# The second pair's gate products moved ahead of the first pair's down products in a mixer and mixture-of-experts layer

## The chip, the cores and the metric

One core of one Trainium2 chip runs the whole program. The metric is the device time of one launch in microseconds (us). Below, PE is TensorE (matrix products), DVE is VectorE, ACT is ScalarE, POOL is GpSimd, and SP is SyncE, which here only issues DMA transfers. Each engine works through its own instructions strictly in the order in which they are written to it.

## The reference

One layer over 1024 tokens of width 1024: a mixer (two kinds of gated linear attention), a layer norm, a mixture of experts, and a second layer norm. The change lies in the mixture of experts, cut here to what matters:

```python
p_top_group, g_idx = lax.top_k(softmax(x @ w_group_router), 1)       # 8 groups
p_top, e_local = lax.top_k(softmax(e_logits_of_that_group), 2)       # 2 of its 8 experts
gates = p_top_group * p_top / sum(p_top)
# for each of 64 experts e, over the rows of x that are sent to it:
h = silu(x_e @ w_gate[e]) * (x_e @ w_up[e])      # 1024 -> 512, twice
y += gates * (h @ w_down[e])                     # 512 -> 1024
out = layer_norm(ALPHA * x + y, ln2_g, ln2_b)
```

## The kernel before

The mixer, the first norm and the router fill the first 545 us. Then `pairs()` walks over the 64 experts in 32 pairs; a pair is two experts, each with up to 64 rows, side by side in the 128 rows of one tile. The six weight matrices of a pair are called units, 2 MB each: two gates (units 6p and 6p+1 of pair p), two ups (6p+2, 6p+3) and two downs (6p+4, 6p+5). All 192 units, 403 MB, come from HBM.

Ten units fit on the chip: four `w1u` and four `w2u` buffers that are used in turn for ever, and two `w3u` buffers (pools `preL` and `preR`) that hold only the first pair's downs, units 4 and 5. `load_after(i)` queues on SP the load that goes into the buffer of unit i, and SP waits there until PE's last product with unit i is done. So units 10 and 11 (second pair's downs) wait for the first pair's gate products, 12 and 13 (third pair's gates) for its ups, 14 and 15 for the second pair's gates, 16 and 17 for the second pair's ups, 18 and 19 for the second pair's downs. Behind units 4 and 5 nothing is loaded; the space of their two buffers is taken over, once the first pair's down products are done, by the pools `home` (tiles `parts` and `rest`) and `ring` (tiles `y`, `rows` and others).

PE's order is written out by hand (`tc.manual_schedule`); the other engines' order comes from the framework's scheduler, except where `order(a, b, ...)` puts a behind b on one engine. For one pair PE does:

- `gp`, the gate products: 16 instructions (8 chunks of the 1024 inputs for 2 experts), then ACT makes `sg` = silu of it;
- `up`, 16 more, then DVE multiplies `sg` by it;
- `hidden`: 4 transposes of `sg` into PSUM (name `tp`), which DVE copies to `hT`;
- `down`, two halves n = 0, 1 of 8 instructions, which ACT and DVE scale into `y` (`scaled`);
- `add_rows` of the pair before, 8 products that add its `y` to the sums of its group of 8 experts (name `cp`).

The rows `xt` of the first two pairs are fetched with an indirect DMA each (`gather`, into `xgs[2]` and `xgs[0]`) and turned on PE (`transposed`), and ACT writes the result. From the third pair on they are picked on PE from the group's rows (`picked`, 24 products a half), which are held as three bf16 tiles in `parts`. `split_rows(g, c, E)` makes these for class c of group g: ACT casts the first (`b0`), engine E subtracts it (`rest`), ACT casts the second (`b1`), E subtracts that into the third (`b2`). Small tables say which row is whose: `trow` and `grow` are spread over the partitions by one product each (`spread_out`), `first_rows` finds a group's first-class rows with three small products, and `adders` makes `adds` from `grow`. `spread` turns vectors of ln2 into the tiles `lns`; numbers 6 and 7 are made inside the first pair. Before the change the first pair was the first pass of the loop, with many `if p == 0`:

```python
            if p == 0:
                spread(6, ps_c, "cp")
                spread(7, ps_c, "cp")
            if p == 0:
                transposed(xgs[0], (0,))
            ...
            hT = hidden(sg)
            ...
                for c in range(4):
                    down(p, yps, hT, n, c)
```

Of the kernel before, what the change touches and what calls it, by code (L numbers as in the profile page):

```python
# [20 lines left out]
D = 1024  # L21
# [38 lines left out]
def mixer_moe_kernel(ctx: ExitStack, tc: tile.TileContext, x_in, xT_in, wf_in, wv_in, wvg_in, wa2_in,  # L60
# [1093 lines left out]
    def turned(products, halves):  # L1154

        xt = xts.rearrange("p (c s) -> p c s", c=KT)
# [9 lines left out]
    def transposed(src, halves=(0, 1)):  # L1166

        sv = src.rearrange("p (k c) -> p c k", c=KT)
        return turned(lambda o, c: PE.transpose(o, sv[:, c], ident), halves)
# [16 lines left out]
    def hidden(sg):  # L1186
# [6 lines left out]
        V.tensor_copy(hT, hp)  # L1193
# [55 lines left out]
    def spread_out(col, n, name, pool):  # L1249

        w = mw.tile([128, n, 128], F32, name="sg", bufs=1)
# [9 lines left out]
    def slot_tokens(g):  # L1261
        return spread_out(tokf[:, GP * g:GP * g + GP], GP, "trow", mw)

    def row_tokens(g):
        return spread_out(rtok[:, 2 * g:2 * g + 2], 2, "grow", ring)
# [8 lines left out]
    def first_rows(g):  # L1274

        tp = ps_x.tile([128, 1], F32, name="tp")
        for q in range(GP - 1):
            col = slice(GP * g + q, GP * g + q + 1)
            m = mw.tile([128, 128], F32, name="own")
# [15 lines left out]
    def split_rows(g, c, E):  # L1295
# [3 lines left out]
        rest = home.tile([128, KT, 128], F32, name="rest", bufs=1)  # L1299
        S.copy(b0, x)  # L1300
        o = E.tensor_tensor(rest, x, b0, OP.subtract)
        if g == 0:
            order(o, evacuated, "the sums of the pair before go first")
        S.copy(b1, rest)
        ends[g] = E.tensor_tensor(b2, rest, b1, OP.subtract)

# [65 lines left out]
    def pairs():  # L1372
# [6 lines left out]
        for p in range(npair):  # L1379
            g, q = divmod(p, GP)  # L1380
            if p == 0:
                gather(xgs[0], sidx[:, 1:2])
                fetch_rows(0, (1,))
            if p == 1:
                for c in (1, 0):
                    split_rows(0, c, V)
            if q == 1:
                for c in range(2):
                    order(gained(G, rows_of[g % 2, c]), ends[g], "the next group's rows go first")
                if g + 1 < NG:  # L1390
                    fetch_rows(g + 1)
            if q > 1 and g + 1 < NG:
                split_rows(g + 1, q - 2, G)
            if 0 < p < last:
# [10 lines left out]
            for u, dst in ((0, gp), (2, up)):  # L1405
                for c in range(KT):
                    if p == last and u == 2 and c == 0:
                        for n in range(2):
                            PE.matmul(sums[g][1][n], own[1], rows_of[g % 2, 1][:, n * 512:(n + 1) * 512], start=False,
                                      stop=False)  # L1410
                    for b in range(2):
                        PE.matmul(dst[64 * b:64 * b + 64], xt[:, c, 64 * b:64 * b + 64], utile[6 * p + u + b][:, c],  # L1412
                                  start=(c == 0), stop=(c == KT - 1))
                for b in range(2):
                    load_after(6 * p + u + b)
                if u == p == 0:
                    count_places()
                    first_rows(0)
                if u == 0:
                    sg = mw.tile([128, FF], F32, name="sg", bufs=1)  # L1420
                    silu = S.activation(sg, gp, AF.Silu)  # L1421
                    if p == last:
                        order(S.activation(mw.tile([128, 1], F32, name="zve"), one1, AF.Sqrt), silu, "one table, then the other")
                    elif p:
                        add_rows(p - 1, adds)
                    if p == last - 1:
                        order(G.drain(), outs[-1], "the rows that are complete go first")
            V.tensor_tensor(sg, sg, up, OP.mult)  # L1428
            if p == 0:
                spread(6, ps_c, "cp")  # L1430
                spread(7, ps_c, "cp")
            if p == 0:
                transposed(xgs[0], (0,))
            elif p < last:
                picked(picks, (0,))
            hT = hidden(sg)
            yps = [ps_g.tile([128, 512], F32, name="gu") if p else ps_c.tile([128, 512], F32, name="cp") for _ in range(2)]
            if 0 < p < last:
                ys[p] = ring.tile([128, 2, D], F32R, name="y")
            for n in range(2) if p < last - 1 else ():  # L1440
                for c in range(4):
                    down(p, yps, hT, n, c)
                if n == 0:
                    if p == 0:
                        xt = transposed(xgs[0], (1,))
                        fetch_rows(0, (0,))
                        trow[:] = [slot_tokens(0)]
                    else:
                        xt = picked(picks, (1,))
                    if q == 2 and g + 1 < NG:  # L1450
                        trow[:] = [slot_tokens(g + 1)]
                if p:
                    scaled(yps, n, gcol[:, p:p + 1], ys[p][:, 0], ys[p][:, 1])
            if p == 0:
                preL.release()
                preR.release()
# [227 lines left out]
```

## Time and profile before

| what | us |
|---|---|
| median of three runs | 1506.78 |
| lowest and highest of them | 1503.84, 1508.77 |
| the profiled execution | 1504.2 |
| its span, first to last instruction | 1502.4 |
| PE busy in it | 1436.2 |

The granted PE clock was 0.998 of full speed. The profile of one execution gives, beside busy times, a row of the 16 DMA engines' busy share in 40 equal slices of 37.6 us, and their throughput in GB/s; a timeline of each engine (start, duration, engine, line, operation, names, and in brackets the idle time before it with what ended it); and sums over stretches that one chooses. A row of the timeline merges like instructions that follow each other, and its duration runs from the first one's start to the last one's end; neighbouring rows overlap by up to 0.1 us, since an engine starts one instruction while the one before drains. An fp32 product of 512 columns counts as two records in the trace (x32 for 16 instructions).

### The profile page before, as it was taken

How to read it: one execution, taken by the hardware profiler on the slowest of the kernel's cores; microseconds unless marked ns; L12 is line 12 of the kernel's file. 1: busy time of each engine (PE TensorE's matmuls, PEld its weight loads, DVE VectorE, ACT ScalarE, POOL GpSimd, SP SyncE). 2: the span in 40 equal slices, each digit the busy share in tenths (PEclk: the TensorE clock that was granted, in tenths of full speed). 3: DMA queues.
4: the chain of work that ended last, by engine and by line, in shares of the span. 5: the costliest groups of instructions: out<-in, count | busy, mean ns of one | idle time of the engine just before them, and what ended most of it. 6: DMA issues, size and time to landing. Idle time of an engine off the chain costs nothing. (4 is left out here: it accounts for less than half of the span.)

```text
span 1502.4 us, 24758 instructions
## 1 busy us (share of the span) xinstructions
PE 1436.2 (96%) x10397; PEld 834.5 (56%) x10397; DVE 627.2 (42%) x1476; ACT 488.6 (33%) x961; POOL 223.2 (15%) x164
## 2 busy tenths in 40 slices
PE   9999999999999999999999999999999999999996
PEld 7888788887888854334344444444343443444432
DVE  6776674838545865141151132133033133114213
ACT  6656553557322423311311311221222221231120
POOL 0000000010012213220320220140140130032000
PEclk9999999999999999999999999999999999999999
DMA  5111111101285278999999999999999999999995
GB/s 184 50 37 43 30 36 37 30 29 45 80 319 198 113 270 356 416 427 427 426 426 427 426 428 424 428 426 425 428 427 428 425 427 427 426 428 425 425 420 213
DMA packets 58293, 445.50 MB, mean 297 GB/s; under 512 B 8916, under 2 KB 17364, under 8 KB 32576
## 3 DMA queue, kind: packets, MB, share of 16 engines
q1 hardware_dynamic: 51184, 430.01, 69.1%
q0 software_dynamic: 4896, 8.84, 1.6%
q10 hardware_dynamic: 2096, 5.01, 0.9%
q8 instruction: 83, 1.36, 0.4%
q14 instruction: 34, 0.28, 0.0%
HBM read 440.24 MB, written 12.58 MB: 301 GB/s over the span
## 5 line engine op out<-in xcount | busy, mean ns | idle before, releaser
L1412 PE MATMUL gu<-w1u,VOA 128*64 128x512 f32 x1024 | 246.1, 595 | 4.4 <-DMA w1u<-in_wu_dram 3.0
L1412 PE MATMUL gu<-w2u,VOA 128*64 128x512 f32 x992 | 237.7, 595 | 11.9 <-DMA w2u<-in_wu_dram 6.5
L1163 ACT ACTIVATE VOA<-tp,cols 128x128 f32<-128x128 f32 x256 | 96.0, 456 | 348.2 <-PE tp L1175 325.4
L1412 PEld LDWEIGHTS gu<-w1u,VOA 128*64 128x64 f32 x1024 | 82.6, 137 | 156.4 <-issue 131.6
L1412 PEld LDWEIGHTS gu<-w2u,VOA 128*64 128x64 f32 x992 | 87.4, 137 | 146.1 <-issue 111.1
L170 PE MATMUL pp<-xl,wh 128*128 128x512 f32 x416 | 165.0, 397 | 0.0
L170 PE MATMUL pp<-xh,wh 128*128 128x512 f32 x416 | 163.7, 393 | 0.6 <-ACT vt L223 0.6
L170 PE MATMUL pp<-xh,wl 128*128 128x512 f32 x416 | 163.3, 393 | 0.0
L1200 DVE SCALAR_TENSOR_TENSOR y<-gu,gcol,y 128x512 fp32r<-128x512 f32 x60 | 45.0, 750 | 220.4 <-ACT y L1199 220.3
L1369 PE MATMUL gu<-w2u,hT 128*64 128x512 f32 x512 | 118.8, 597 | 12.4 <-ACT VOA L1163 11.6
L1369 PE MATMUL gu<-w1u,hT 128*64 128x512 f32 x480 | 109.6, 598 | 12.4 <-ACT VOA L1163 11.6
L1175 PEld LDWEIGHTS <-parts 128*128 128x128 bf16 x1248 | 69.9, 98 | 48.8 <-issue 48.8
L170 PEld LDWEIGHTS pp<-xh,wh 128*128 128x128 f32 x416 | 78.1, 188 | 18.1 <-ACT vt L223 1.0
L1199 ACT ACTIVATE y<-gu,gcol 128x512 fp32r<-128x512 f32 x60 | 41.1, 686 | 141.4 <-PE gu L1369 141.4
L170 PEld LDWEIGHTS pp<-xl,wh 128*128 128x128 f32 x416 | 78.1, 188 | 16.3 <-issue 0.2
L170 PEld LDWEIGHTS pp<-xh,wl 128*128 128x128 f32 x416 | 78.2, 188 | 15.7
L1428 DVE TENSOR_TENSOR sg<-sg,gu 128x512 f32<-128x512 f32 x32 | 22.0, 687 | 148.8 <-PE gu L1412 148.8
L1421 ACT ACTIVATE sg<-gu 128x512 f32<-128x512 f32 x31 | 18.5, 598 | 196.0 <-PE gu L1412 196.0
L1369 PEld LDWEIGHTS gu<-w2u,hT 128*64 128x64 f32 x512 | 40.5, 136 | 73.3 <-issue 55.3
L1175 PE MATMUL tp<-pick,parts 128*128 128x128 bf16 x1248 | 80.1, 219 | 0.8 <-DVE hT L1193 0.8
L1369 PEld LDWEIGHTS gu<-w1u,hT 128*64 128x64 f32 x480 | 34.6, 136 | 65.4 <-issue 49.0
L1319 DVE TENSOR_SCALAR adds<-grow,tokf 128x256 fp32r<-128x256 f32 x31 | 21.1, 681 | 111.9 <-PE cp L1330 111.9
(354 smaller groups left out, 1959.8 us busy)
## 6 DMA issues: line engine op xcount, KB each, us to landing
w1u<-in_wg_dram SPq DMA_DIRECT2D x30, 2048.0 KB, 27.9
w1u<-in_wu_dram SPq DMA_DIRECT2D x30, 2048.0 KB, 28.3
w2u<-in_wg_dram SPq DMA_DIRECT2D x30, 2048.0 KB, 26.0
w2u<-in_wu_dram SPq DMA_DIRECT2D x30, 2048.0 KB, 29.0
w1u<-in_wd_dram SPq DMA_DIRECT2D x30, 2048.0 KB, 28.6
w2u<-in_wd_dram SPq DMA_DIRECT2D x28, 2048.0 KB, 28.0
wr<-in_wf_dram SPq DMA_DIRECT2D x36, 256.0 KB, 2.9
w1u<-in_wg_dram SPq DMA_DIRECT2D x8, 1024.0 KB, 21.8
```

What stands on the lines that cost most here:

```text
L170: PE.matmul(ps, w[:, k], x_[:, k, ts], start=(k == 0 and j == 0), stop=(k == KT - 1 and j == len(terms) - 1))
L1163: S.activation(xt[:, c], tp[:, i], AF.Identity, bias=cols[:, 42 + c:43 + c], scale=cols[:, 34 + c:35 + c])
L1175: PE.matmul(o, part[:, c], m, start=(i == 0), stop=(i == len(ms) - 1))
L1199: S.mul(yh[:, ns], yps[n], gate_col)
L1200: return V.scalar_tensor_tensor(yl[:, ns], yps[n], gate_col, yh[:, ns], op0=OP.mult, op1=OP.subtract)
L1319: V.tensor_scalar(m, grow[0], tokf[:, p:p + 1], None, op0=OP.is_equal)
L1369: PE.matmul(yps[n][64 * b:64 * b + 64], hT[:, c, 64 * b:64 * b + 64], utile[6 * p + 4 + b][:, c, n * 512:(n + 1) * 512], start=(c == 0), s ...
L1412: PE.matmul(dst[64 * b:64 * b + 64], xt[:, c, 64 * b:64 * b + 64], utile[6 * p + u + b][:, c], start=(c == 0), stop=(c == KT - 1))
L1421: silu = S.activation(sg, gp, AF.Silu)
L1428: V.tensor_tensor(sg, sg, up, OP.mult)
```

## The change

The first two pairs are taken out of the loop and written out with their steps interleaved: first gate, first up, second gate, first down, second up, second down. The rows of the second pair are now turned between the first gate and the first up, into the tile that held the first pair's source. `count_places` and the three products of `first_rows(0)` stand inside the first up, `hidden` and the table `trow` inside the second gate, the table `grow` inside the second up. For these two tables the spread source lies in the first pair's `xt` tile, which is read no more, and no longer in `sg`. `split_rows` of group 0 now uses two engines: class 0 on DVE, with the tile `rows` as its `rest`, class 1 on POOL; POOL's clearing of `rows` is gone. `spread` 6 and 7 stand behind the second up. The two halves of `picked` for the third pair stand around the last half of the second down, with `add_rows(0)` ahead of them. From the third pair on each pair's order is as before.

```diff
+        xt = transposed(xgs[2])
+        gather(xgs[0], sidx[:, 1:2])
+        fetch_rows(0, (1,))
+        gp = ps_g.tile([128, FF], F32, name="gu")
+        rows_by(0, 0, gp, xt)
+        sg, _ = gate(0, gp)
+        xt1 = transposed(xgs[0], xgs[2])
+        up = ps_g.tile([128, FF], F32, name="gu")
+        firsts = first_rows_of(0)
+        rows_by(0, 2, up, xt, {2: count_places, 4: lambda: next(firsts), 6: lambda: next(firsts, None)})
+        fetch_rows(0, (0,))
+        V.tensor_tensor(sg, sg, up, OP.mult)
...
+        rows_by(1, 0, gp, xt1, {4: first_hidden})
+        hT = hT[0]
+        sg, _ = gate(1, gp)
+        yps = [ps_c.tile([128, 512], F32, name="cp") for _ in range(2)]
+        for n in range(2):
+            for c in range(4):
+                down(0, yps, hT, n, c)
+        preL.release()
+        preR.release()
...
+        evacuated = all_scaled(0, yps)
+        low, low_end = split_rows(0, 0, V, rows_of[1, 1])
+        order(low, evacuated, "the sums of the pair before go first")
+        split_rows(0, 1, G)
+        up = ps_g.tile([128, FF], F32, name="gu")
+        rows_by(1, 2, up, xt1, {4: lambda: grow.append(row_tokens(0, xts[:, 512:768]))})
+        order(low_end, V.tensor_tensor(sg, sg, up, OP.mult), "the hidden rows go first")
+        wide = [spread(j, ps_c, "cp") for j in (6, 7)]
+        hT = hidden(sg, wide[0])
+        order(wide[0], low_end, "the parts go first")
+        first_rows(1)
+        next_rows(0)
+        adds = adders(0)
+        picks = pickers(2)
...
+        for n in range(2):
+            for c in range(4):
+                down(1, yps, hT, n, c)
+            if n == 0:
+                add_rows(0, adds)
+                picked(picks, (0,))
+            scaled(yps, n, gcol[:, 1:2], ys[1][:, 0], ys[1][:, 1])
+        xt = picked(picks, (1,))
...
+        for p in range(2):
+            for u in range(4, 6):
+                load_after(6 * p + u)
```

`rows_by(p, u, dst, xt, between)` is the old loop over chunks and experts with the two `load_after` behind it, and calls `between[c]` behind chunk c. `next_rows(g)` scales the group's rows on POOL (`gained`, four instructions) and then fetches the next group's rows (`fetch_rows`, two gathers).

What stands on PE from the first pair's transposes of the hidden rows on, before: `gu<-w2u` are the second pair's gate and up, `cp<-w3u` the first pair's down, `tp<-tokf` is `first_rows`.

```order
L1191 MATMUL tp<-cst,sg 128x128 x4
L1369 MATMUL cp<-w3u,hT 64x512 x8
L1169 MATMUL tp<-cst,VOA 128x128 x4
L1255 MATMUL tp<-sg,one_6401 128x512
L1369 MATMUL cp<-w3u,hT 64x512 x8
L1255 MATMUL tp<-sg,one_6401 128x256
L1281 MATMUL tp<-tokf,own 128x1 x3
L1412 MATMUL gu<-w2u,VOA 64x512 x16
L1330 MATMUL cp<-y,adds 128x512 x8
L1412 MATMUL gu<-w2u,VOA 64x512 x16
```

And after, from the start of the second pair's gate to its down (`gu<-w1u,hT`):

```order
L1390 MATMUL gu<-w2u,VOA 64x512 x10
L1191 MATMUL tp<-cst,sg 128x128 x4
L1257 MATMUL tp<-VOA,one_6401 128x512
L1390 MATMUL gu<-w2u,VOA 64x512 x6
L1377 MATMUL cp<-w3u,hT 64x512 x16
L1390 MATMUL gu<-w2u,VOA 64x512 x10
L1257 MATMUL tp<-VOA,one_6401 128x256
L1390 MATMUL gu<-w2u,VOA 64x512 x6
L1369 MATMUL cp<-cst,cols 128x128 x8
L1191 MATMUL tp<-cst,sg 128x128 x4
L1289 MATMUL tp<-tokf,own 128x1 x3
L1377 MATMUL gu<-w1u,hT 64x512 x8
```

The second gate has moved ahead of the first down, and `spread` and `first_rows(1)` stand directly ahead of the second down.

What stands on DVE from the scaling of the first pair's sums on, before (`sg<-sg,gu` and `hT<-tp` are the second pair's):

```order
L1200 SCALAR_TENSOR_TENSOR y<-cp,gcol,y 128x512 x2
L1319 TENSOR_SCALAR adds<-grow,tokf 128x256
L1301 TENSOR_TENSOR rest<-VOA,parts 128x1024
L1305 TENSOR_TENSOR parts<-rest,parts 128x1024
L1301 TENSOR_TENSOR rest<-VOA,parts 128x1024
L1305 TENSOR_TENSOR parts<-rest,parts 128x1024
L1319 TENSOR_SCALAR adds<-grow,tokf 128x256
L1428 TENSOR_TENSOR sg<-sg,gu 128x512
L1193 COPY hT<-tp 128x512
```

And after, at the same place (the last row is the third operand of `first_rows(1)` and one for later):

```order
L1202 SCALAR_TENSOR_TENSOR y<-cp,gcol,y 128x512 x2
L1310 TENSOR_TENSOR rows<-VOA,parts 128x1024
L1327 TENSOR_SCALAR adds<-grow,tokf 128x256
L1449 TENSOR_TENSOR sg<-sg,gu 128x512
L1312 TENSOR_TENSOR parts<-rows,parts 128x1024
L1371 COPY VOA<-cp 128x4x128
L1193 COPY hT<-tp 128x512
L1371 COPY VOA<-cp 128x4x128
L1288 TENSOR_SCALAR own<-place,places 128x128 x2
```

Class 1 has left DVE for POOL; the last subtraction of class 0 and the two copies of `spread` now stand around the copy to `hT`.

What stands on ACT from the copy of `trow` on, before:

```order
L1258 COPY trow<-tp 128x512
L1300 CAST parts<-VOA 128x1024
L1199 ACTIVATE y<-cp,gcol 128x512 x2
L1258 COPY grow<-tp 128x256
L1300 CAST parts<-VOA 128x1024
L1304 CAST parts<-rest 128x1024
L1421 ACTIVATE sg<-gu 128x512
```

And after:

```order
L1260 COPY trow<-tp 128x512
L1399 ACTIVATE sg<-gu 128x512
L1309 CAST parts<-VOA 128x1024
L1201 ACTIVATE y<-cp,gcol 128x512 x2
L1309 CAST parts<-VOA 128x1024
L1311 CAST parts<-rest 128x1024
L1311 CAST parts<-rows 128x1024
L1260 COPY grow<-tp 128x256
```

The second pair's silu now stands ahead of the casts, and the copy of `grow` behind all four.

More of the change, by code (lines that the diff above doesn't have):

```diff
@@ L1184, in product, with hidden @@
         return sg
-    def hidden(sg):
+    def hidden(sg, ahead=None):
         hp = ps_x.tile([128, 4, 128], F32, name="tp")
@@ L1192, in hidden @@
         hT = mw.tile([128, 4, 128], F32, name="hT", bufs=1)
-        V.tensor_copy(hT, hp)
+        turn = V.tensor_copy(hT, hp)
+        if ahead:
+            order(ahead, turn, "the hidden rows go first")
         return hT
@@ L1274, in first_rows, with first_rows_of @@
     def first_rows(g):
+        for _ in first_rows_of(g):
+            pass
+    def first_rows_of(g):
         tp = ps_x.tile([128, 1], F32, name="tp")
@@ new lines, in gate, with all_scaled, next_rows @@
+        def gate(p, gp):
+            sg = mw.tile([128, FF], F32, name="sg", bufs=1)
+            return sg, S.activation(sg, gp, AF.Silu)
+        def all_scaled(p, yps):
+            ys[p] = ring.tile([128, 2, D], F32R, name="y")
+            return [scaled(yps, n, gcol[:, p:p + 1], ys[p][:, 0], ys[p][:, 1]) for n in range(2)][-1]
+        def next_rows(g):
+            for c in range(2):
+                order(gained(G, rows_of[g % 2, c]), ends[g], "the next group's rows go first")
+            if g + 1 < NG:
+                fetch_rows(g + 1)
@@ L1387, in pairs @@
             if q == 1:
[L1388 to L1391, printed above, removed]
+                next_rows(g)
             if q > 1 and g + 1 < NG:
                 split_rows(g + 1, q - 2, G)
-            if 0 < p < last:
+            if p < last:
                 picks = pickers(p + 1)
@@ L1404, in pairs @@
             up = ps_g.tile([128, FF], F32, name="gu")
[L1405 to L1434, printed above, removed]
+            rows_by(p, 0, gp, xt)
+            sg, silu = gate(p, gp)
+            if p == last:
+                order(S.activation(mw.tile([128, 1], F32, name="zve"), one1, AF.Sqrt), silu, "one table, then the other")
+                for n in range(2):
+                    PE.matmul(sums[g][1][n], own[1], rows_of[g % 2, 1][:, n * 512:(n + 1) * 512], start=False, stop=False)
+            else:
+                add_rows(p - 1, adds)
@@ L1435, in pairs @@
+            if p == last - 1:
+                order(G.drain(), outs[-1], "the rows that are complete go first")
+            rows_by(p, 2, up, xt)
+            V.tensor_tensor(sg, sg, up, OP.mult)
+            if p < last:
                 picked(picks, (0,))
             hT = hidden(sg)
-            yps = [ps_g.tile([128, 512], F32, name="gu") if p else ps_c.tile([128, 512], F32, name="cp") for _ in range(2)]
-            if 0 < p < last:
+            yps = [ps_g.tile([128, 512], F32, name="gu") for _ in range(2)]
@@ L1439, in pairs @@
+            if p < last:
                 ys[p] = ring.tile([128, 2, D], F32R, name="y")
@@ L1443, in pairs @@
                 if n == 0:
[L1444 to L1449, printed above, removed]
+                    xt = picked(picks, (1,))
                     if q == 2 and g + 1 < NG:
                         trow[:] = [slot_tokens(g + 1)]
[L1452 to L1456, printed above, removed]
[L1457 to L1464 removed]
+                scaled(yps, n, gcol[:, p:p + 1], ys[p][:, 0], ys[p][:, 1])
             if p > last - 2:
```

69 lines of the change are left out of this document (39 added, 30 removed).

## The prediction, made before the changed kernel was run

> **What bounds the kernel now.** I read the slices of the page first: PE and DMA.
>
> ```profile
> PE 1436.2 (96%) x10397; PEld 834.5 (56%) x10397; DVE 627.2 (42%) x1476; ACT 488.6 (33%) x961; POOL 223.2 (15%) x164
> ...
> DMA  5111111101285278999999999999999999999995
> GB/s 184 50 37 43 30 36 37 30 29 45 80 319 198 113 270 356 416 427 427 426 426 427 426 428 424 428 426 425 428 427 428 425 427 427 426 428 425 425 420 213
> ```
>
> PE looks full at 96%, but from the seventeenth slice (602 us) on DMA stands at 9 and the rate at 416 to 428 GB/s, up to the last slice: there the stream of weights sets the time, and PE follows it. So whatever happens behind 602 us is hidden, and a microsecond counts only if the stream itself starts earlier or later. Sums over stretches around that point show where it is not full:
>
> ```profile
> 560.00:580.00 20.00, 18.88 (x100) 8.73 (x98) 6.03 (x15) 6.03 (x12) 2.93 (x3) 1.00 1.00 423
> 580.00:587.50 7.50, 7.50 (x37) 3.00 (x34) 5.83 (x6) 4.54 (x6) 0.99 (x1) 1.00 0.50 122
> 587.50:607.00 19.50, 18.72 (x123) 8.13 (x123) 8.10 (x6) 6.69 (x11) 12.42 (x5) 1.00 0.97 413
> 607.00:609.00 2.00, 2.00 (x12) 0.60 (x10) 0.00 (x0) 1.39 (x2) 0.85 (x2) 1.00 0.80 221
> 609.00:700.00 91.00, 87.92 (x486) 36.91 (x484) 29.91 (x66) 19.40 (x39) 20.10 (x11) 1.00 1.01 426
> ```
>
> The last two columns are DMA share and GB/s. There are two holes, 580 to 587.5 (122 GB/s) and 607 to 609 (221 GB/s), and none behind. SP's timeline says which loads end them:
>
> ```profile
> 586.08 0.80 SPq L800 DMA_DIRECT2D w2u<-in_wu_dram  x2
> 595.14 0.81 SPq L800 DMA_DIRECT2D w2u<-in_wd_dram  x2
> 606.59 0.80 SPq L800 DMA_DIRECT2D w1u<-in_wg_dram  x2
> ...
> 633.91 0.80 SPq L800 DMA_DIRECT2D w2u<-in_wg_dram  x2
> ```
>
> They are units 14/15 (behind the second gate), 16/17 (second up), 18/19 (second down) and 24/25 (third down). Two units are 4.2 MB, 9.8 us at 427 GB/s. 14 to 17 fill 587.5 to 607; then the queue is empty for a moment, and 18/19, issued at 606.59, start the stream that never stops again. **The time therefore hangs on one instant, T, the issue of 18/19, which is the end of the second pair's down products on PE. T is 606.59 now.** What is gained ahead of T is lost again if the queue is empty at T.
>
> **The change, on PE.** The rows of its timeline that I price with:
>
> ```profile
> 548.94 7.09 PE L1412 MATMUL gu<-w1u,VOA 128*64 128x512 f32 x32
> ...
> 564.87 2.05 PE L1361 MATMUL cp<-cst,cols 128*128 128x128 f32 x16
> ...
> 567.19 0.64 PE L1191 MATMUL tp<-cst,sg 128*128 128x128 f32 x4
> ...
> 572.82 1.02 PE L1255 MATMUL tp<-sg,one 128*128 128x512 f32 x2
> 573.77 3.65 PE L1369 MATMUL cp<-w3u,hT 128*64 128x512 f32 x16
> 577.36 0.70 PE L1255 MATMUL tp<-sg,one 128*128 128x256 f32 x2
> ...
> 585.99 2.10 PE L1330 MATMUL cp<-y,adds 128*128 128x512 f32 x8
> ...
> 595.05 1.51 PE L1175 MATMUL tp<-pick,parts 128*128 128x128 bf16 x24
> ...
> 606.39 7.04 PE L1412 MATMUL gu<-w1u,VOA 128*64 128x512 f32 x32
> ```
>
> The first up ends at 564.9 before. Between first gate and first up stand now the eight transposes of the second pair instead of the tables' products; these go inside the up, where their operands are ready. I take 564.9 again, and nothing for this edit. Then the second gate 7.0, hidden 0.6, `trow` 0.95: 573.4. So 14/15 are issued 12.7 us earlier than at 586.08, and the first hole closes. First down, two halves of 3.6: 580.6. Second up 7.0 and `grow` 0.55: 588.1, where 16/17 are issued, 7 us earlier. The stream then runs 580 to 590 with 14/15 and to 599.6 with 16/17, and is empty until T.
>
> If nothing else were late, PE would go on with `spread` 6 and 7 (1.9), hidden (0.6), the copy to `hT` and `first_rows(1)`, together to 591.3. From the second down's start to T it is 3.6 + 2.05 (`add_rows`) + 1.4 (one half of the picks) + 3.6 = 10.7 us. T would be 602.0, and the kernel 4.6 us faster. That is the bound below.
>
> **What is late next.** The second down's start hangs on DVE, POOL and ACT, whose orders have changed more than PE's. ACT, DVE and POOL before:
>
> ```profile
> 577.46 2.05 ACT L1300 CAST parts<-VOA 128x1024 bf16<-128x1024 f32 x1 [2.40 <-PE cp L1369]
> 579.41 1.25 ACT L1199 ACTIVATE y<-cp,gcol 128x512 fp32r<-128x512 f32 x2
> 580.56 0.36 ACT L1258 COPY grow<-tp 128x256 f32<-128x256 f32 x1
> ...
> 588.66 1.05 ACT L1304 CAST parts<-rest 128x1024 bf16<-128x1024 f32 x1 [1.93 <-DVE rest L1301]
> ```
>
> ```profile
> 565.08 0.69 DVE L1428 TENSOR_TENSOR sg<-sg,gu 128x512 f32<-128x512 f32 x1 [6.52 <-PE gu L1412]
> 566.06 2.05 DVE L1363 COPY VOA<-cp 128x512 f32<-128x512 f32 x2 [0.29 <-PE cp L1361]
> 567.96 0.68 DVE L1193 COPY hT<-tp 128x512 f32<-128x512 f32 x1
> ...
> 581.45 0.34 DVE L1319 TENSOR_SCALAR adds<-grow,tokf 128x256 fp32r<-128x256 f32 x1
> 581.71 2.02 DVE L1301 TENSOR_TENSOR rest<-VOA,parts 128x1024 f32<-128x1024 f32 x1
> 585.25 1.22 DVE L1305 TENSOR_TENSOR parts<-rest,parts 128x1024 bf16<-128x1024 f32 x1 [1.52 <-ACT parts L1304]
> ...
> 589.74 2.47 DVE L1305 TENSOR_TENSOR parts<-rest,parts 128x1024 bf16<-128x1024 f32 x1 [1.11 <-ACT parts L1304]
> 592.14 2.45 DVE L1319 TENSOR_SCALAR adds<-grow,tokf 128x256 fp32r<-128x256 f32 x1
> ```
>
> ```profile
> 588.77 5.66 POOL L1245 TENSOR_TENSOR VOA<-VOA 128x1024 f32<-128x1024 f32 x2 [7.69 <-DVE rest L1301]
> 594.40 4.71 POOL L1246 TENSOR_TENSOR VOA<-VOA 128x1024 f32<-128x1024 f32 x2
> 604.92 2.66 POOL L1301 TENSOR_TENSOR rest<-VOA,parts 128x1024 f32<-128x1024 f32 x1 [5.81 <-ACT parts L1300]
> 608.73 2.13 POOL L1305 TENSOR_TENSOR parts<-rest,parts 128x1024 bf16<-128x1024 f32 x1 [1.15 <-ACT parts L1304]
> ```
>
> The first cast waits for the end of the first down (577.46 now), whose buffer `parts` takes over. That end moves to 580.6, 3.2 us later, while the second pair's silu product is wanted 7 us earlier. ACT's own order then gives: cast b0 of class 0 to 582.65, two `y` to 583.8, cast b0 of class 1 to 585.8. Now ACT waits for POOL's `rest` of class 1, 2.66 us: 588.5. Then cast b1 of class 1 to 589.5, cast b1 of class 0 to 590.5, and only then `grow`, 590.85.
>
> DVE's order puts `adds` (it reads `grow`) ahead of the second pair's `sg`, and so the product that PE is waiting for starts at 591.2 although its up ended at 588.1: `sg` to 591.9, b2 of class 0 (1.22) to 593.1, one copy of `spread` 1.05, `hT` at 594.9, the other copy 1.05, one `own` 0.3. PE starts the second down at 596.4 at best, because `first_rows(1)` with that `own` stands ahead of it. With 10.7 us this gives T = 607.1, 0.5 later than now. Break-even is a start at 595.9.
>
> That sum takes POOL and DVE as independent. The rows say they are not: the same DVE instruction took 1.22 us with POOL idle and 2.47 beside POOL's L1245, `adds` 0.34 and 2.45, and it ended at 594.59, just behind POOL's pair (588.77 + 5.66 = 594.43); that pair was longer too, 5.66 against 4.71 for the next. So these two kinds wait for each other whole. After the change DVE's `rest` of class 0 (584.6 to 586.65) holds back POOL's `rest` 0.7 us, which moves ACT's chain to `grow` at 591.5; `adds` then waits for POOL's b2 of class 1 (2.13, 590.3 to 592.45), so `sg` ends at 593.3; and DVE's b2 of class 0 meets the first `gained` product (2.36, to 594.9) and ends at 596.0. With the copies and `own`: second down at 599.1, **T = 609.8, 3.2 us later than now**. I take this end, since the pairs that meet are those whose meetings the rows show; 0.5 is kept for the range. The Trainium skill, page SBUF — State Buffer, section Who interferes with whom, has this as a rule: a DVE instruction with two SBUF inputs, or in a 2-port mode, and a GpSimd one that reads SBUF exclude each other for a whole instruction, the first to issue winning. By that rule T is 609.8 and without it 607.1; the 2.47 and 2.45 above agree with it.
>
> **Behind T.** The third gate used to follow the second down at once; now the second half of the picks (1.45) stands between, so 20/21 and later loads come 1.45 later against T. The queue has room: some 1.5 us pass from issue to full flow (586.08 to 587.5), so 18/19 to 22/23 occupy it until about 637.5 now (608.1 + 3 x 9.8), and 24/25, issued at 633.91, have 2.1 us in hand. SP, with the same loads in the same order, gets no new wait. POOL's gathers of the second group move from 578.8 behind the `gained` four, to about 604; ACT casts them ahead of the last four copies of the third pair's `xt`, but this cast waits for the picks anyway (611.2). Their landing:
>
> ```profile
> rows<-x1d,gidx POOLq DMA_INDIRECT x1, 3.8
> ...
> VOA<-x1d,gidx POOLq DMA_INDIRECT x5, 10.2
> ```
>
> In an empty queue, as there will be until T, 3.8: landed at 608.4, no cost. POOL's missing memset is worth nothing; the tables' new place is hidden by the up products.
>
> **Sum.** The profiled execution: 1504.2 + 3.2 = 1507.4 (span 1502.4 to 1505.6). It lies 2.6 below the median of the runs shown; for the median 1506.78 + 3.2 = 1510.0.
>
> **Rivals.** First, the forecast's chain without the mutual waits, T = 607.1: 1507.3. For it: whether two instructions meet is a matter of tenths. Against: POOL is busy almost without break from 586 to 603. Second, the other side: DVE and ACT run ahead of my chain, because `parts` is free before the whole first down is done. Only unit 4's reads hold it; if the cast could start with the half n = 1, at 577, everything moves 3.6 us: T 603.5 without the mutual waits and 606.2 with them, 1503.7 to 1506.4. Against: the row of 577.46 shows the cast waiting for exactly the last down product. It decides from a cast start of 580.1 on without the mutual waits, 577.4 with them. Third, slower still: DVE loses one more meeting (2.3: 1512.3), or the second group's rows land in 10.2 us, at 614.7 instead of 608.4. Then ACT's cast and the first of the last `xt` copies end at 617.1, the fifth chunk of the third gate waits 2.4 us, 24/25 come 3.2 + 1.45 + 2.4 later, more than the 2.1 in hand allow by 1.75, and the time is 1511.7.
>
> **How the numbers follow.** About 0.3%, 4.5 us, is what a measurement here can tell from no change. Chances: forecast 0.42, of which 0.05 past 4.5; no mutual waits 0.26, all within; earlier start 0.14, of which 0.04 past -4.5 (only where nothing at all is late); slower still 0.18, of which 0.13 past 4.5. Faster 0.04, same 0.78, slower 0.18. The range goes from the bound below, 1502.2, to both parts of the third rival, 1510.0 + 2.3 + 1.75 = 1514.
>
> **What would show it.** Right: 14/15 near 573.4 and 16/17 near 588, no hole at 580, but one of about 12 us from 600 to 611 before 18/19; PE idle some 8 us ahead of `first_rows(1)` and the second down, with DVE named; `sg` of the second pair starting 4 us behind its up; DVE's b2 of class 0 above 2 us. Wrong: 18/19 issued before 606, or a hole behind 612, which would say that PE, not T, is the limit there, or `grow` copied before 588.

## The result: 0.5% slower, one meeting and one slow clock more than the forecast

The changed kernel takes 1513.66 us (median of 6 runs, 1513.29 to 1515.25) against 1506.20 for the kernel before (6 runs): ratio 1.0052, 95% interval 1.0042 to 1.0063. That is 7.5 us slower where 3.2 were forecast: past the 4.5 us that were called no change, and 0.3 us inside the upper end of the range. The profiled execution took 1513.93 (span 1512.1), 9.7 more than that of before, which lies 2.0 below its median. Its two rows of slices on DMA, 37.8 us each:

```profile
DMA  5111011101284278899999999999999999999994
GB/s 183 51 36 43 30 43 30 32 27 45 84 342 181 112 290 374 323 421 426 426 428 425 427 427 425 428 428 425 426 428 426 426 428 425 426 428 426 425 420 192
```

The seventeenth slice (605 to 643 us) fell from 416 to 323 GB/s; behind it the stream is as full as before. SP's timeline of the same loads, and the sums over stretches (the last three columns are PE's granted clock, DMA share, GB/s):

```profile
574.62 0.80 SPq L800 DMA_DIRECT2D w2u<-in_wu_dram  x2
589.13 0.80 SPq L800 DMA_DIRECT2D w2u<-in_wd_dram  x2
613.90 0.80 SPq L800 DMA_DIRECT2D w1u<-in_wg_dram  x2
...
643.17 0.81 SPq L800 DMA_DIRECT2D w2u<-in_wg_dram  x2
```

```profile
580.00:587.50 7.50, 7.50 (x36) 2.50 (x34) 3.33 (x3) 5.17 (x4) 0.75 (x1) 1.00 1.02 433
587.50:600.00 12.50, 5.15 (x32) 3.66 (x28) 7.71 (x8) 2.26 (x3) 11.34 (x5) 0.78 0.99 404
600.00:613.90 13.90, 12.57 (x68) 5.84 (x69) 5.22 (x8) 2.19 (x5) 5.51 (x4) 0.83 0.22 68
613.90:640.00 26.10, 24.81 (x146) 10.74 (x147) 3.83 (x6) 9.38 (x14) 4.79 (x2) 1.00 0.97 400
640.00:700.00 60.00, 57.78 (x336) 24.61 (x334) 25.57 (x59) 14.38 (x31) 17.17 (x9) 1.00 1.01 424
```

The hole at 580 is closed (433 GB/s for 122). In its place there is one at 600, 13.9 us at 68 GB/s, and it ends at T = 613.90, the issue of units 18/19, not at 609.8. The third column from the right is new: PE's clock, 1.00 in every stretch before, is 0.78 and 0.83 around the hole. PE, DVE and POOL in the same place:

```profile
594.13 0.92 PE L1191 MATMUL tp<-cst,sg 128*128 128x128 f32 x4 [3.04 <-DVE sg L1449]
594.85 0.85 PE L1289 MATMUL tp<-tokf,own 128*128 128x1 f32 x4
601.33 0.58 PE L1289 MATMUL tp<-tokf,own 128*128 128x1 f32 x2 [5.64 <-DVE own L1288]
601.85 5.05 PE L1377 MATMUL gu<-w1u,hT 128*64 128x512 f32 x16
606.82 2.11 PE L1338 MATMUL cp<-y,adds 128*128 128x512 f32 x8
608.78 1.51 PE L1175 MATMUL tp<-pick,parts 128*128 128x128 bf16 x24
610.22 3.65 PE L1377 MATMUL gu<-w1u,hT 128*64 128x512 f32 x16
```

```profile
592.29 1.10 DVE L1327 TENSOR_SCALAR adds<-grow,tokf 128x256 fp32r<-128x256 f32 x1 [4.79 <-ACT grow L1260]
593.31 0.67 DVE L1449 TENSOR_TENSOR sg<-sg,gu 128x512 f32<-128x512 f32 x1
593.91 2.78 DVE L1312 TENSOR_TENSOR parts<-rows,parts 128x1024 bf16<-128x1024 f32 x1
...
597.52 0.67 DVE L1193 COPY hT<-tp 128x512 f32<-128x512 f32 x1
598.12 1.06 DVE L1371 COPY VOA<-cp 128x512 f32<-128x512 f32 x1
599.04 4.54 DVE L1288 TENSOR_SCALAR own<-place,places 128x128 f32<-128x128 bf16 x2
```

```profile
593.20 5.69 POOL L1247 TENSOR_TENSOR VOA<-VOA 128x1024 f32<-128x1024 f32 x2
598.86 4.64 POOL L1248 TENSOR_TENSOR VOA<-VOA 128x1024 f32<-128x1024 f32 x2
603.65 1.03 POOL L1146 DMA_INDIRECT rows<-x1d,gidx  x1 [0.15 <-issue]
604.98 0.99 POOL L1146 DMA_INDIRECT VOA<-x1d,gidx  x1 [0.30 <-issue]
```

Two rows are not in the forecast. `own` of the second group took 4.54 us for two, the first to 601.28 and the second to 603.58, each just behind one of POOL's two L1248; PE waited for the first of them 5.64 us. And the first half of the second down took 5.05 us where the second half, the same 16 records, took 3.65: the trace records the granted clock at 0.5 from 594.46 to 604.70, a mean of 0.53 in this stretch (same columns as above):

```profile
594.00:605.00 11.00, 5.23 (x18) 3.01 (x20) 10.12 (x10) 0.00 (x0) 10.54 (x6) 0.53 0.63 267
```

### The profile page after: what moved, and what is told of

It is laid out like the page before. It is cut to its first block, busy times and chain, and to the rows that moved or that the text cites. A ratio compares the mean times of both kernels' runs of the same rounds, so it can differ in the third digit from the quotient of the medians.

```text
span 1512.1 us, 24758 instructions
## 1 busy us (share of the span) xinstructions
PE 1439.6 (95%) x10397; PEld 830.9 (55%) x10397; DVE 626.5 (41%) x1474; ACT 488.8 (32%) x961; POOL 227.4 (15%) x165
## 5 line engine op out<-in xcount | busy, mean ns | idle before, releaser
L1390 PEld LDWEIGHTS gu<-w2u,VOA 128*64 128x64 f32 x992 | 83.0, 137 | 148.8 <-issue 123.5
L1377 PE MATMUL gu<-w2u,hT 128*64 128x512 f32 x512 | 119.5, 605 | 12.4 <-ACT VOA L1163 11.6
L1377 PE MATMUL gu<-w1u,hT 128*64 128x512 f32 x480 | 112.1, 604 | 11.7 <-ACT VOA L1163 11.6
```

The lines of the kernel that those rows point to most:

```text
L1377: PE.matmul(yps[n][64 * b:64 * b + 64], hT[:, c, 64 * b:64 * b + 64], utile[6 * p + 4 + b][:, c, n * 512:(n + 1) * 512], start=(c == 0), s ...
```

## The experiments

Four series. The runs of each shared the kernel before on one chip (medians 1505.92 for e1 to e4, 1505.86 for e5 to e8, 1505.90 for e9 to e11, 1505.23 for e12), so what is compared between series is the distance to it. Since the start of a trace moves by a us or two, T is also given from the first gate product on. Two views were to be told apart. In the first, T alone sets the time, and T is set by DVE's order and by its meetings with POOL (instructions of the two that wait for each other). In the second, something behind T, or the early loads, counts too.

**e1: the second group's place moved behind the first half of the picks.**

```diff
-        first_rows(1)
-        next_rows(0)
...
                 picked(picks, (0,))
+                first_rows(1)
+                next_rows(0)
```

> The changed kernel, with first_rows(1) (and next_rows(0) behind it) moved from ahead of the second down to behind the first half of the picks, so that PE no longer waits for the third own operand; DVE's order up to hT stays. Theory (the time hangs on T, the issue of 18/19, one for one; the changed kernel had T 613.9 against 606.6 before): PE starts the second down when hT is copied, 598.2 instead of 601.85, T 609.5 (610.8 if PE's clock is still down in the first half), time 1509 to 1510.5, that is 3 to 4.5 under the changed kernel. Rival (the later stages of the third pair set the time, 20/21 and behind, not T): no more than 1.5 under the changed kernel.

1512.03 us, ratio 1.0043 (1.0031 to 1.0055); T 612.49, later than the 609.5 or 610.8 expected. 0.9 us of that lies ahead of the edit: in this trace the clock was at 0.5 from 548.11 to 551.52, the first gate took 8.30 for 7.09, and 16/17 came at 589.99 for 589.13. `own` no longer stood ahead of the second down, which started 2.7 us earlier than in the changed kernel, but ran slowly, 5.41 for 3.65, in a stretch of half clock from 595.9 to 602.7:

```profile
599.14 5.41 PE L1377 MATMUL gu<-w1u,hT 128*64 128x512 f32 x16 [3.44 <-issue]
```

**e2: besides, `hT` ahead of b2 on DVE.** `hidden` puts both copies of `spread` and b2 behind `hT`.

```diff
-        hT = hidden(sg, wide[0])
-        order(wide[0], low_end, "the parts go first")
+        hT = hidden(sg, wide + [low_end])
+        for o in wide:
+            order(o, low_end, "the parts go first")
```

> As e1, and on DVE the copy to hT goes ahead of class 0's last subtraction (b2) and of both spread copies. Theory (T): sg ends at 594.0 as in the changed kernel, hT at 595.6, second down at 595.7, PE idle 3 us instead of 3 and 5.6, clock not down, T 606.8, time 1506 to 1507, the kernel before within 1. Rival: POOL's and DVE's mutual waits come back at the picks (b2 is late), T 609 or more, 1509.

1508.90 us, ratio 1.0020 (1.0011 to 1.0029); T 610.15 for 606.8. The second down came as expected, right behind `hT`, with the clock just fallen (0.5 from 594.80 to 601.63):

```profile
594.02 0.72 PE L1191 MATMUL tp<-cst,sg 128*128 128x128 f32 x4 [3.05 <-DVE sg L1449]
595.58 6.64 PE L1377 MATMUL gu<-w1u,hT 128*64 128x512 f32 x16 [0.83 <-issue]
```

So a single wait of 3.05 us cost 3.0 us once more, in the work behind it. That is nearly all that missed: 606.8 + 3.0 = 609.8.

**e3: besides, the silu product `sg` and `hT` ahead of `adds`,** then the copies, then b2, so that PE's wait for `sg` goes.

```diff
-        hT = hidden(sg, wide + [low_end])
+        hT, turn = hidden(sg, wide, both=True)
+        adds, added = adders(0, turn)
         for o in wide:
-            order(o, low_end, "the parts go first")
-        adds = adders(0)
+            order(o, added, "the adders go first")
+            order(low_end, o, "the sums' banks are freed first")
```

> As e2, and on DVE the product sg and hT go ahead of adds as well, which waits for the copy of grow; then adds, both spread copies, b2. Theory (T): sg starts at the end of the second up (589), hT at 592.3, second down at 592.4, PE without idle time there, T 603.5 to 604, time 1503 to 1504, 3 under the kernel before and 10 under the changed one. Rival (the casts of group 0 start 4 us later than before since they wait for the first down, and b2 is what the picks wait for): T no better than 606.6, 1506.

T 605.74, 2 us later than expected since PE waited 1.61 for `own` again; the clock stayed at 1.00 up to T. Yet the time is 1509.12, ratio 1.0021 (1.0006 to 1.0035), over 12 runs from 1503.80 to 1514.31. The profiled one (1512.47, one of the longer ones; the others have no trace) shows a hole behind T:

```profile
616.30 2.02 ACT L1309 CAST parts<-VOA 128x1024 bf16<-128x1024 f32 x1 [9.82 <-DMA VOA<-x1d,gidx]
```

```profile
618.73 5.26 PE L1393 MATMUL gu<-w1u,VOA 128*64 128x512 f32 x16 [7.98 <-ACT VOA L1163]
```

The second group's rows, asked for at 605.41, landed at 616.22 behind 18/19, which were issued 0.3 us later. ACT stood with its cast, and the third gate with ACT; behind this wait of 7.98 us the clock was at 0.5 once more, from 615.18 to 622.01. This is the gather of the third rival, in a kernel where T comes early enough to overtake it; it is the only run in which T does not tell the time.

**e4: the changed kernel with 14/15 held back to the end of the first down.**

```diff
-            for b in range(2):
+            for b in range(2) if (p, u) != (1, 0) else ():
...
+        for b in range(2):
+            after(load_after(6 + b), end, "held back until the first down is done")
```

> The changed kernel, with the loads 14/15 held back until the first down is done (581.3 instead of 574.6), so that the hole ahead of them partly opens again; PE, T and all else the same. Theory (only T counts, since the queue is empty at T anyway): the time of the changed kernel within 1, 1513 to 1514.5, T 613.9. Rival (each hole in the stream of weights counts by itself): about 3 slower, 1516.5.

1512.03 us, ratio 1.0043 (1.0031 to 1.0055), not slower than the changed kernel: 6.1 above the kernel before for 7.5, a little less than the "within 1" that was expected, with intervals that overlap. 14/15 were issued at 581.37 for 574.62, and T was 613.70, from the first gate 64.46 for 64.51: what the change gains in the first hole is worth nothing.

The next four were to part the two rows that were not in the forecast.

**e5: PE kept busy in its wait.** Five products that nobody uses, between the second and third product of `first_rows(1)`:

```diff
-        first_rows(1)
+        firsts = first_rows_of(1)
+        next(firsts)
+        for _ in range(5):
+            PE.matmul(yps[0], one1.to_broadcast([128, 128]), xts[:, 0:512], start=True, stop=True)
+        next(firsts, None)
```

> The changed kernel with five additional products of 128x512 on PE (results unused, overwritten by the second down) between the second and the third product of the second group's place, where PE waited 5.64 us in the changed kernel. Theory (the wait let the granted clock fall to 0.5, and that alone made the first half of the second down 5.05 us instead of 3.65): PE is busy from about 595 to 600.2, the clock stays at 1.00, the first half takes 3.65, T (the issue of units 18/19) comes at 612.5 instead of 613.90, the time 1.4 lower: about 1512.3. Rival (the half is long for another reason, say DVE's and POOL's traffic beside it): the half stays near 5 us, T 613.9, time 1513.7. Rival (the 3.04 us wait ahead of the hidden transposes is enough for the clock to fall): the clock is still 0.5 in spite of the added products, T 613.9 or a little later.

1511.32 us, ratio 1.0038 (1.0025 to 1.0052). The first half of the second down took 3.65 and T was 612.31, 1.6 earlier, but the clock did not stay at 1.00: it fell at 595.15 and was back at 598.56, while the added products ran, so that the down met a full clock:

```profile
594.12 0.72 PE L1191 MATMUL tp<-cst,sg 128*128 128x128 f32 x4 [3.04 <-DVE sg L1449]
594.67 0.50 PE L1289 MATMUL tp<-tokf,own 128*128 128x1 f32 x4
595.04 6.24 PE L1457 MATMUL gu<-VOA,one 128*128 128x512 f32 x10
601.34 0.38 PE L1289 MATMUL tp<-tokf,own 128*128 128x1 f32 x2
601.65 3.65 PE L1377 MATMUL gu<-w1u,hT 128*64 128x512 f32 x16
```

The wait of 3.04 alone brought the clock down, then; the second wait, 5.64 without products, only kept it down.

**e6: `own` moved out of POOL's way,** into the first down, where DVE and POOL have nothing to do.

```diff
+        firsts = first_rows_of(1)
         for n in range(2):
             for c in range(4):
                 down(0, yps, hT, n, c)
+                if (n, c) in ((0, 3), (1, 1)):
+                    next(firsts, None)
...
-        first_rows(1)
```

> The changed kernel with one thing moved: the three products of the second group's place, with DVE's own masks, stand between the halves of the first down (574 to 581, where neither DVE nor POOL has work), instead of ahead of the second down. POOL's gained and the gathers stay where they are. Theory (DVE's third own met POOL's gained, and PE stood behind it): no own is left at 599, PE starts the second down right behind hT's copy, at about 598.2 instead of 601.85. T is 610.2 if the first half still runs at half clock (5.05), 608.8 if it doesn't; time 1510.0 or 1508.6. DVE's other meetings (adds 1.10, b2 2.78) stay. Rival (T isn't set by own; hT or add_rows ends the wait anyway): T stays above 612 and the time above 1512. Rival (the products between the halves of the first down delay PE there): 16/17 issued 1 us or more after 589.1.

1511.12 us, ratio 1.0036 (1.0022 to 1.0050). T 612.75 looks like the rival, but this trace starts 1.3 us later (first gate product at 550.70 for 549.39): from there to T it is 62.05 for 64.51, 2.5 less. PE waited 3.17 for `hT` and no longer for `own`; 16/17 came 1.15 later against the first gate, since the three products now stand in the first down: the last rival holds as well, and takes back some of the gain. That is also why T, 611.44 without the later start, missed the 610.2 that was expected at half clock.

**e7: both, with two added products ahead of the hidden transposes and three behind.**

```diff
+        busy = lambda n: [PE.matmul(yps[0], one1.to_broadcast([128, 128]), xts[:, 0:512], start=True, stop=True) for _ in range(n)]
+        busy(2)
         hT = hidden(sg, wide[0])
+        busy(3)
```

> As the one before (own masks and their products between the halves of the first down), and PE kept busy in both waits ahead of the second down: two added products of 128x512 (1.02 us each) ahead of the hidden transposes, three behind them, results overwritten. Theory (what is left over the unchanged kernel is the clock, then the waits): the clock stays at 1.00, the second down's first half takes 3.65, T 608.8 (598.2 + 10.7), time about 1508.6. That is the chain of the forecast (T 609.8) less its own 0.3 and the half clock. Rival (the clock falls all the same): T 610.2 and 1510.0. Rival (added products delay the hidden transposes): transposes later than 594.5.

1509.42 us, ratio 1.0025 (1.0014 to 1.0036): 3.6 us slower than the kernel before. PE's longest wait is 1.23 us and the clock 1.00 throughout:

```profile
592.00:602.00 10.00, 7.88 (x35) 4.07 (x35) 6.92 (x6) 2.26 (x3) 8.84 (x5) 1.00 0.96 380
```

Without the two rows that the forecast lacked, the order costs about what the forecast said, 3.2. That they agree so closely is in part luck: `own` and its products, which the forecast's chain holds, are gone from it here, and standing in the first down they make 16/17 1.14 us later. For the same reason T, 610.07 without the later start of this trace, came 1.3 us behind the 608.8 that was expected.

**e8: e3, with `own` as in e6, and the gather of the second group's first class ahead of POOL's gained four.**

```diff
+        _, high_end = split_rows(0, 1, G)
...
+        ahead = gather(rows_of[1, 0], gidx[:, 2:3])
+        order(ahead, high_end, "the group's own rows go first")
...
-                order(gained(G, rows_of[g % 2, c]), ends[g], "the next group's rows go first")
+                order(gained(G, rows_of[g % 2, c]), ends[g] if g else ahead, "the next group's rows go first")
```

> The kernel of e3 (second pair's silu product and hT ahead of adds, copies and b2 on DVE) with the second group's place and own masks between the halves of the first down, and the gather of the second group's first rows ahead of POOL's gained four instead of behind them (its index is known by then). Theory (T decides, and e3's late gather was all that cost it time behind T): second down starts near 592.7, no wait for own, T about 603.5 to 604.5 against 606.59 in the kernel before; the gather lands by 605; no hole behind T; time 1502.5 to 1504, 2 to 4 us faster than the kernel before, without e3's spread. Rival (something else binds: the first down's buffers, b2 of class 0 that the picks read, POOL's longer gained): T 606 or later and the time like before, 1506. Rival (the gather still lands late because 16/17 are in flight when it is issued): a hole behind T of several us and 1509 to 1512.

1511.61 us, ratio 1.0044 (1.0029 to 1.0058), a miss for the theory. The second down started at 593.65, the gather landed at 604.93, but the picks waited 6.62 us for b2 of class 0:

```profile
596.41 9.63 DVE L1312 TENSOR_TENSOR parts<-rows,parts 128x1024 bf16<-128x1024 f32 x1
```

```profile
595.67 4.71 POOL L1247 TENSOR_TENSOR VOA<-VOA 128x1024 f32<-128x1024 f32 x2
600.33 4.63 POOL L1248 TENSOR_TENSOR VOA<-VOA 128x1024 f32<-128x1024 f32 x2
```

DVE's instruction of 1.22 us ended 1.09 behind POOL's last (604.96). It was shut out for four POOL instructions in a row, and the wait let the clock fall as well (first half of the picks and second half of the down 2.53 and 5.11).

**e9: e6 with the gained four held until DVE has emptied the second pair's sums, both gathers ahead of them.**

```diff
+            evacuated = scaled(yps, n, gcol[:, 1:2], ys[1][:, 0], ys[1][:, 1])
+        for c in range(2):
+            after(gained(G, rows_of[0, c]), evacuated, "held until DVE has emptied the second pair's sums")
```

> The kernel of e6 (the second group's place and DVE's own masks between the halves of the first down) with POOL's gained four held until DVE has emptied the second pair's sums (about 610), and the two gathers of the second group ahead of them. DVE's b2 of class 0 then has no gained beside it. Theory (instructions of these two kinds wait for each other, and b2's 2.78 us were a meeting): b2 takes 1.2 to 1.25 us, hT's copy starts 1.5 us earlier against the second gate than in e6, PE waits 1.6 us instead of 3.17 ahead of the second down. adds still meets POOL's b2 of class 1 (1.10). T is 1.5 earlier than e6's against 12/13 and the time 1509.6; if the clock no longer falls, 1.4 less again: 1508.2. With the two added products of e7 not needed, this is the forecast's chain without most of its meetings. Rival (b2 is long for its own sake): 2.78 and no gain over e6's 1511.1.

1509.04 us, ratio 1.0019 (1.0010 to 1.0029). b2 took 1.22, PE's second wait fell from 3.17 to 1.56, and the clock fell all the same (0.5 from 596.77 to 603.59):

```profile
597.29 1.22 DVE L1312 TENSOR_TENSOR parts<-rows,parts 128x1024 bf16<-128x1024 f32 x1
```

```profile
597.43 1.13 PE L1191 MATMUL tp<-cst,sg 128*128 128x128 f32 x4 [2.95 <-DVE sg L1452]
600.11 5.37 PE L1377 MATMUL gu<-w1u,hT 128*64 128x512 f32 x16 [1.56 <-issue]
```

**e10: e8 with the gained four held in the same way.**

> The kernel of e8, in which DVE's b2 of class 0 stood still for 9.63 us beside POOL's four gained, with these four held until DVE has emptied the second pair's sums, and both gathers ahead of them. Theory (POOL's run of gained shut DVE out for its whole length, and that alone cost e8 its gain): b2 takes 1.25, the first picks start at once behind add_rows, near 599.3, no PE wait of over 1 us after the hidden transposes, the clock stays at 1.00, T 604.4 to 604.8 (12/13 plus 38.4) against 606.59 in the kernel before; both gathers land by 605; time 1503.5 to 1504.5, about 2 us faster than the kernel before. Rival (gained, now 605 to 615, meets DVE's or POOL's later work and makes a hole behind T): a PE wait in the third gate or up and a time of 1506 or more.

1502.82 us, ratio 0.9982 (0.9973 to 0.9991): faster than the kernel before. With b2 at 1.22 and no wait above 0.83 us, PE goes through to T = 604.36 at full clock:

```profile
593.71 3.65 PE L1380 MATMUL gu<-w1u,hT 128*64 128x512 f32 x16 [0.83 <-ACT grow L1260]
597.29 2.11 PE L1341 MATMUL cp<-y,adds 128*128 128x512 f32 x8
599.24 1.51 PE L1175 MATMUL tp<-pick,parts 128*128 128x128 bf16 x24
600.68 3.65 PE L1380 MATMUL gu<-w1u,hT 128*64 128x512 f32 x16
604.27 1.51 PE L1175 MATMUL tp<-pick,parts 128*128 128x128 bf16 x24
```

**e11: e10 with `spread` 7 behind the hidden transposes.**

```diff
-        wide = [spread(j, ps_c, "cp") for j in (6, 7)]
+        wide = [spread(6, ps_c, "cp")]
...
+        wide.append(spread(7, ps_c, "cp"))
```

> The kernel of e10 with the last table's products on PE parted: those of spread 6 ahead of the second pair's hidden transposes, those of spread 7 behind them, under hT's copy. Theory: the transposes start 1.0 earlier if sg is done (sg ends 0.7 behind the up, spread 6 takes 1.0), hT 0.8 earlier, and T 0.8 earlier than e10's: 603.6 to 604.0, time about 1503. Rival (spread 7's copy, now last on DVE, holds back the sums' banks that add_rows wants): add_rows waits and nothing is gained over e10.

1501.67 us, ratio 0.9976 (0.9966 to 0.9987), the fastest version. From the first gate to T it is 53.92 for e10's 54.80; the intervals of the two overlap, so the 0.9 between them is shown by the trace and not by the times.

**e12: e8 with two memsets of 128x1 behind each of the gained four,** which stay where they were.

```diff
+                    o = G.tensor_tensor(rows_of[0, c], rows_of[0, c], w, op)
+                    order(o, turn, "in turn")
+                    for _ in range(2):
+                        turn = G.memset(gap, 0.0)
+                        order(turn, o, "in turn")
```

> The kernel of e8, with two memsets of a scratch column (128x1, they read nothing) behind each of POOL's four gained instructions; nothing else differs. In e8 DVE's b2 of class 0 was issued 0.74 us behind the first of the four and ended 1.09 us behind the last, 9.63 us in all, while in the changed kernel the same instruction was let in between the first and the second (2.78). Theory A (DVE is shut out for as long as POOL's instructions follow each other without a break, and a break of an instruction that reads no SBUF lets it in): b2 takes 2.5 to 3.0, the first picks start by 600, the clock stays at 1.00, T 604.4 to 606, time 1503.5 to 1506. Theory B (b2 stands for another reason until the four are done, or such a break is too short): b2 9 us or more, T 613.7 or later, time 1511.6 as in e8.

1503.47 us, ratio 0.9988 (0.9979 to 0.9996), against 1.0044 for e8. The same b2 at the same place, 0.75 us behind POOL's first:

```profile
596.82 2.71 DVE L1313 TENSOR_TENSOR parts<-rows,parts 128x1024 bf16<-128x1024 f32 x1
```

```profile
596.07 2.37 POOL L1413 TENSOR_TENSOR VOA<-VOA 128x1024 f32<-128x1024 f32 x1
598.37 0.26 POOL L1416 MEMSET gap<- 128x1 f32 x2
598.59 3.16 POOL L1413 TENSOR_TENSOR VOA<-VOA 128x1024 f32<-128x1024 f32 x1
```

So it was POOL's unbroken run that shut DVE out in e8: with the run parted, b2 was let in behind the first of the four. Whether the memsets do this because they read nothing, or any break would, is not shown. Nor does an unbroken run always shut DVE out: in the changed kernel, e1, e4, e5, e6 and e7 the same four followed each other as closely, and b2, issued beside the first, was let in behind it (2.77 to 2.78).

All profiled executions together, us:

| kernel | T | time | time − T | first gate to T | against before | median against before |
|---|---|---|---|---|---|---|
| before | 606.59 | 1504.20 | 897.6 | 57.65 | | |
| changed | 613.90 | 1513.93 | 900.0 | 64.51 | +6.9 | +7.5 |
| e1 | 612.49 | 1512.01 | 899.5 | 63.46 | +5.8 | +6.1 |
| e2 | 610.15 | 1508.22 | 898.1 | 60.87 | +3.2 | +3.0 |
| e3 | 605.74 | 1512.47 | 906.7 | 56.64 | −1.0 | +3.2 |
| e4 | 613.70 | 1511.44 | 897.7 | 64.46 | +6.8 | +6.1 |
| e5 | 612.31 | 1511.54 | 899.2 | 62.93 | +5.3 | +5.5 |
| e6 | 612.75 | 1511.12 | 898.4 | 62.05 | +4.4 | +5.3 |
| e7 | 611.47 | 1509.36 | 897.9 | 60.68 | +3.0 | +3.6 |
| e8 | 613.70 | 1511.60 | 897.9 | 64.20 | +6.6 | +5.8 |
| e9 | 612.48 | 1510.29 | 897.8 | 61.56 | +3.9 | +3.1 |
| e10 | 604.36 | 1501.90 | 897.5 | 54.80 | −2.9 | −3.1 |
| e11 | 602.31 | 1500.96 | 898.7 | 53.92 | −3.7 | −4.2 |
| e12 | 604.71 | 1502.94 | 898.2 | 54.80 | −2.9 | −1.8 |

But for e3 with its late gather, the stretch from the first gate to T tells the median within 1.1 us. Two falls of the clock, outside what the edits touch, stand in these columns. In the traces of e1, e3 and e9 it was at 0.5 for 3.41 us at the first gate, which took 8.30, 7.68 and 7.80 for 7.09, so their stretch to T is 0.6 to 1.2 longer. In those of the changed kernel, e1 and e5 it fell for 3.41 us in the last pair as well, whose down took 8.78 for 7.65 to 7.92 elsewhere: their time − T is 899.2 to 900.0, that of the others but e3 897.5 to 898.7.

## Why the prediction fell short

**What held.** That the time hangs on T: but for e3, T moved over 11.6 us in these kernels and the rest of the execution stayed within 2.5. That closing the first hole brings nothing: e4. The chain on ACT, POOL and DVE up to `grow`: the cast started at 581.49, behind the last down product, so the second rival (an earlier cast) falls; the copy of `grow` ended at 592.25 for 591.5. The three meetings that the sum counted: POOL's `rest` 3.21 for 2.66 beside DVE's, `adds` 1.10 beside POOL's b2, and b2 2.78 beside gained, which e9 takes away (1.22); so the first rival (no mutual waits) falls. `sg` started 4.2 us late (593.31, its up ended at 589.1), and PE waited 3.04 and 5.64 (8 foreseen). 14/15 and 16/17 were 1.2 and 1.0 us later than forecast, of which 0.45 is the later start of this trace. Behind T, 24/25 came 29.27 us after it for 27.32, and the slack hid it: e4 and e10 with the same 29.27 have a time − T of 897.7 and 897.5, the kernel before 897.6.

**What failed.** T was 613.90 for 609.8. Two terms of the sum make 3.3 of these 4.1; the other 0.8 are `own`, which started at 599.04 where the sum has it at about 598.7 (this trace starts 0.45 later), and the last product of `first_rows(1)`, which stood on PE for 0.5 between `own` and the second down, where the sum left 0.1 to 0.2. The `own` of the second group in the trace of before:

```profile
578.21 0.51 DVE L1280 TENSOR_SCALAR own<-place,places 128x128 f32<-128x128 bf16 x2 [2.44 <-PE tp L1281]
```

- "The copies and `own`": the forecast gave `own` 0.3 and listed meetings for `adds`, `rest` and b2 only. `own` met L1248, and PE stood until 601.28 for it, 1.9 us more. In the trace of before, the `own` of the first groups ran in 0.28 to 0.40 us with nothing beside it on POOL but a memset, which reads nothing, so it showed no meeting. But `adds`, of the same operation (TENSOR_SCALAR), did show one there (2.45 for 0.34), and the forecast used that row. This is the one more meeting of the third rival, which had 2.3 for it. e6 took it away: 2.5 less from first gate to T, 2.2 in the distance of the medians.
- "With 10.7 us this gives T": the 3.6 for a half of the down is a row at full clock, and no row of before has PE waiting 3 us here. The forecast itself had PE idle 8 us and never asked what PE would be like afterwards. The half took 5.05, 1.4 more; e5 gives 3.65 and T 1.6 earlier.

With both out, e7 is 3.6 us slower than the kernel before for the forecast's 3.2, in part by luck as said above. The second part of the third rival, late rows, did not happen in the changed kernel (its gathers were issued 9 and 10 us ahead of T, landed at 607.06 and 608.84, and the third gate is one row of 7.09), but does in e3.

What the order moves on PE is not what loses the time. e10 and e11 keep it, and give DVE the product that PE waits for first, move `own` to where DVE is idle, the gathers ahead of POOL's gained and these behind T: 3 to 4 us faster than before, near the bound of 4.6 that the forecast gave where nothing is late.

## What to carry to other kernels

Where a forecast moves work into a stretch in which two engines exclude each other, list every instruction of both that now falls into it, the small ones too, and price each that PE waits for with a whole instruction of the other engine, not with its own duration. If the new order makes PE wait some 3 us ahead of the work that sets the end, price that work at half clock; shorter waits let the clock fall in some executions. A long run of POOL instructions belongs behind the instant on which the time hangs, or must be broken up, and a gather ahead of the loads that are queued there.

## What the runs showed of the hardware

- PE's clock fell to 0.5 in all seven kernels in which PE waited 2.95 to 3.05 us for `sg` (changed, e1, e2, e4, e5, e6, e9), and in none around this place where its longest wait was 1.61 (e3, up to T), 1.23 (e7) or 0.83 (e10, e12). Each stretch of 0.5 there lasted 3.41, 6.83 or 10.24 us, one, two or three times 3.41, the longest where a second wait of 5.64 or 5.55 followed (changed, e4). No safe length can be read from this: ahead of the first gate, behind waits of 1.85 to 2.04 us that every kernel has, the clock fell in three of the fourteen traces (e1, e3, e9), and in the last pair, behind waits of 0.86 and 0.8 with four transposes between them, which every kernel has too, in three as well (changed, e1, e5). The Trainium skill, page TensorE: Matmul & The Clock Gate, Part 1: The HAM clock gate, has a free-running window of about 3.4 us that throttles to half after an idle window and releases after a busy one: the lengths agree. The same page of the Trainium skill, in its section HAM oscillation — how this bites in real kernels, has idle gaps above about 3.4 us as the danger (about 3 us in its closing table); here 3.0 were enough each time, and less at times.
- One DVE instruction of 1.22 us took 9.63 when four POOL instructions followed each other without a break (e8), 2.78 and 2.71 when it was let in behind the first (changed, e12). The page SBUF — State Buffer of the Trainium skill, section Who interferes with whom, has the first to issue hold the shared port for one whole instruction; in e8 DVE was still shut out when POOL's next instruction began, three times over. Why it was let in between two POOL instructions in the changed kernel, e1, e4, e5, e6 and e7 and not in e8 stays open; that memsets between them let it in was shown at this place alone.
- Two gathers of 128 rows landed 3.4 and 3.9 us after their issue with no load queued (changed), and 10.8 us after it where two loads of 2 MB were issued 0.3 us later (e3).
